# A decoder step on one core: the MLP by Strassen's seven products, the embedding ahead of it, the gate by halves

## The chip, the cores and the metric

One core of a Trainium2 chip. The metric is device time in microseconds (us) from the start to the end of one execution. The engines are named as in the profile: PE (matrix products), DVE and POOL (element by element), ACT (functions, and copies), SP (issues the transfers).

## What is computed

One decoder layer for 1024 prompt tokens and 32 sample tokens, all fp32, width 1024. Attention over a window, a recurrent branch and their mix come first and are not touched. The part that changes:

```python
x = x + mix
hmid = relu(rmsnorm(x, norm2_g) @ w_up)         # 1024 -> 4096
x = x + (hmid * hmid) @ w_down                  # 4096 -> 1024
gate = sigmoid(rmsnorm(x, ple_norm_g) @ w_ple_gate)
x = x + gate * (p @ w_ple)                      # p: 256 wide
```

## The kernel before

Everything is kept feature-major: a matrix of 1024 features by T = 1056 tokens is KT = 8 tiles of 128 features, `X[j]` being the residual. An fp32 product is made of two parts of each operand, high and low: `product` (L234) issues three matmuls for each tile k of the inner dimension, high weights by high tokens (L239), high by low (L240), low by high (L241). `piece` and `linear` (L243, L252) run one group of weights (128 output features) over three chunks of 352 tokens. `weights` hands out a group: it splits the next one (ACT casts the high part, L141, DVE subtracts for the low part, L142), and SP loads the one after that.

Side work is spread by the class `Flow`: `flow.later(n, f)` and `flow.run(generator, n)` put work off by n chunks, and `flow.step()` after each chunk emits what has come due. What is emitted stands in its engine's queue in that order, and each engine works its queue in order.

- **w_out and second norm.** `put_x1` (L1008) adds each chunk to `X`; `with_gain` (L983) squares it and sums the squares on POOL, and splits x times gain into `x1a` and `x1b` (ACT, then DVE). The division by the norm is put off: the MLP works on x times gain, the sums (`mean_square`, L997) come due two chunks into the MLP, and POOL multiplies `X` by them in the first quarter (L1039).
- **MLP.** Four quarters f, each of 8 groups up and 8 groups down, 24 matmuls of 352 columns for a chunk. `put_up` (L1029): ACT relu, POOL square, ACT square to the high part, DVE low part (L1035). `put_down` (L1048): DVE adds the product to `X` (L1050); in the last quarter it multiplies by the norm and calls `with_gain` again, with `x2a` and `x2b`.
- **Gate.** For each row j: 72 matmuls of `w_ple_gate` (`put_gate`, L1118), then 18 of the embedding `w_ple` (`put_y`, L1123), and `write_out` (L1100) turns `X[j]` on PE (L1107), copies it on ACT and sends it. It is put off by one chunk (`flow.run(write_out(...), 1)`, L1155), and a chunk of row j + 1 is emitted ahead of it.

PSUM has two pools of four banks, `pm` for the main products and `po` for the rest.

Of the kernel before, what the change touches and what calls it, by code (L numbers as in the profile page):

```python
# [13 lines left out]
F32 = mybir.dt.float32  # L14
# [12 lines left out]
CH = [(c * CW, CW) for c in range(3)]  # L27
H, G, HD, WIN = 8, 2, 64, 128
# [5 lines left out]
UL = 384                  # width of a row of the biases by distance, u = 255 - distance  # L34
# [26 lines left out]
class Flow:  # L61
    """Work beside the main products, emitted a number of chunks of theirs later."""
# [8 lines left out]
    def run(self, steps, chunks=0):  # L71
        """steps: a generator that yields how many chunks to wait."""
# [17 lines left out]
def trunk(ctx: ExitStack, tc: tile.TileContext, I, O):  # L90
# [25 lines left out]
    def chunk_tmp(tag):  # L116
        return late.tile([P, CW], F32, tag=tag, name=tag, bufs=2)
# [74 lines left out]
    def use_w_ple(j):  # L192
# [5 lines left out]
        def split(raw):  # L198
            w = big.tile([P, 4, P], F32R, tag=("e7", "e0")[j % 2], name="wple")
# [24 lines left out]
    for f in range(FF // D):  # L224
        for i in range(KT):
            use_w(I["w_up"][0], (8 * f + i) * P)
        for j in range(KT):
            use_w(I["w_down"][0], j * P, r0=f * D)
# [28 lines left out]
    def rsqrt(r, ms, u):  # L257
        """r = -2 / sqrt(ms): a first value by logarithm and exponential, then one Newton step."""
# [9 lines left out]
    # -------------------------------------------------------------- constants  # L268
# [7 lines left out]
    # ------------------------------------------------- x, normalised, turned  # L276
# [84 lines left out]
    # --------------------------------------------------------------- k, v, q  # L361
# [61 lines left out]
    def window_out(last, new, which):  # L423
        """The new keys or values, feature-major, to the windows."""
# [32 lines left out]
    # ------------------------------------------------- biases by distance  # L457
# [21 lines left out]
    def biases():  # L479
        # [query, key] views of the biases: distance query + 128 - key  # L480
# [5 lines left out]
        # the samples' rows are (sequence, token, head of the group)  # L486
# [17 lines left out]
    # ------------------------------------------------------ start, keys, values  # L504
# [77 lines left out]
    # A group's values: high parts in the columns of its own partitions, low parts in the others.  # L582
# [22 lines left out]
    # ---------------------------------------------- attention of the prompt  # L605
    def attend():
# [40 lines left out]
        def values(g, b, parts):  # L647
            """High and low values' sums stand on the two halves of the partitions."""
# [36 lines left out]
    # ---------------------------------------------- attention of the samples  # L685
# [76 lines left out]
    # ------------------------------------------- state and decay rates  # L762
    # softplus(-lambda) = 2 atanh(s / (2 - s)) + max(-lambda, 0), s = sigmoid(-|lambda|)
# [73 lines left out]
        # The r and i gates: the input's high part stands on a block's half of the partitions, its low  # L837
        # part on the other half, so a product over all of them takes both.
# [353 lines left out]
```

## Time and profile before

| what | us |
|---|---|
| median of 3 runs (1695.31 to 1698.9) | 1698.87 |
| the profiled execution, its span | 1695.9 |
| PE busy, of the span | 1644.0 (97%) |
| DVE busy | 715.0 (42%) |
| ACT busy | 654.1 (39%) |
| POOL busy | 421.4 (25%) |
| MLP, first matmul of up to last of down | 824 to 1562 |
| gate and embedding, to the end | 1563 to 1696 |

The span is what the profiler saw between the first and the last instruction; the median of the runs is 3.0 us above it. A row of the trace gives start, length, engine, line, operation, output<-inputs and shape; in brackets stands how long the engine had been idle before it, and what released it. The length of a single matmul is its way through the array; successive starts give the time that each costs.

### The profile page before, as it was taken

The page shows a single profiled execution, that of the slowest core. Times are in us where ns is not written, and L with a number is a line of the kernel's source. Part 1 is how long each engine was busy: PE and PEld are TensorE (multiplying, and loading weights), DVE is VectorE, ACT ScalarE, POOL GpSimd, SP SyncE. Part 2 cuts the span into 40 slices and gives each one's busy share as a digit, 9 for nine tenths or more (in the row PEclk, how much of TensorE's full clock was granted, in tenths as well). Part 3 has the DMA queues.
Part 4 walks back from the last instruction along what each step waited for, and adds up shares of the span by engine and source line. Part 5 has one row for each costly group of instructions (what it writes and reads, how often), then busy time and mean ns, then how long its engine had stood idle before and what let it go on. Part 6 is the DMA issues. An engine that isn't in the chain of part 4 may idle for free.

```text
span 1695.9 us, 24877 instructions
## 1 busy us (share of the span) xinstructions
PE 1644.0 (97%) x10283; PEld 1625.5 (96%) x10283; DVE 715.0 (42%) x1155; ACT 654.1 (39%) x1177; POOL 421.4 (25%) x435
## 2 busy tenths in 40 slices
PE   6889999989899999999999999999999999999998
PEld 5889999889899999999999999999999999999998
DVE  5697665574641153333344224222222222355533
ACT  5555656888892223332232013310231013222322
POOL 4462216344530002234453002200120002144000
PEclk9999999999999999999999999999999999999999
DMA  5422112111111123322211111111111111111222
GB/s 169 63 91 67 61 58 79 29 41 44 43 52 50 29 74 103 101 76 80 60 41 48 50 51 38 50 50 40 49 50 45 43 50 41 48 50 54 64 76 61
DMA packets 174570, 100.48 MB, mean 59 GB/s; under 512 B 17396, under 2 KB 171140, under 8 KB 174440
## 3 DMA queue, kind: packets, MB, share of 16 engines
q1 hardware_dynamic: 174456, 98.88, 20.3%
q8 instruction: 81, 1.33, 0.3%
q14 instruction: 33, 0.27, 0.1%
HBM read 88.32 MB, written 11.55 MB: 59 GB/s over the span
## 4 chain that ended last, share of the span: by engine, by line
PE 90%; DVE 5%; DMA 2%; ACT 2%; issue 1%; SPq 0%; ACTq 0%; DVEq 0%
PE m L239 28%; PE m L241 28%; PE m L240 28%; DMA rev<-by_dist 2%; PE m L654 1%; PE o L642 1%; DVE qh L452 1%; DVE xhl L844 1%; DVE hn L265 0%; PE o L239 0%; PE o L240 0%; PE o L241 0%; PE o L619 0%; PE o L620 0%; PE o L1107 0%
## 5 line engine op out<-in xcount | busy, mean ns | idle before, releaser
L239 PE MATMUL m<-xa,wh 128*128 128x352 f32 x912 | 298.8, 328 | 0.0
L240 PE MATMUL m<-xb,wh 128*128 128x352 f32 x912 | 295.9, 324 | 1.1 <-DVE xb L333 1.0
L241 PE MATMUL m<-xa,wl 128*128 128x352 f32 x912 | 295.8, 324 | 0.0
L241 PE MATMUL m<-uh,wl 128*128 128x352 f32 x768 | 248.2, 323 | 0.0
L239 PE MATMUL m<-x1a,wh 128*128 128x352 f32 x768 | 247.9, 323 | 0.0
L239 PE MATMUL m<-uh,wh 128*128 128x352 f32 x768 | 247.7, 323 | 0.0
L240 PE MATMUL m<-ul,wh 128*128 128x352 f32 x768 | 247.6, 322 | 0.0
L240 PE MATMUL m<-x1b,wh 128*128 128x352 f32 x768 | 246.3, 321 | 0.0
L241 PE MATMUL m<-x1a,wl 128*128 128x352 f32 x768 | 246.3, 321 | 0.0
L141 ACT CAST wh<-wraw 128x1024 fp32r<-128x1024 f32 (+1 forms) x126 | 128.2, 1018 | 278.4 <-PE m L240 278.0
L142 DVE TENSOR_TENSOR wl<-wraw,wh 128x1024 fp32r<-128x1024 f32 (+1 forms) x133 | 161.5, 1215 | 145.0 <-ACT wh L141 124.9
L1033 POOL TENSOR_TENSOR rl<-rl 128x352 f32<-128x352 f32 x96 | 81.6, 850 | 544.2 <-ACT rl L1032 544.2
L1035 DVE TENSOR_TENSOR ul<-rl,uh 128x352 fp32r<-128x352 f32 x96 | 68.4, 713 | 256.7 <-POOL rl L1033 256.7
L240 PEld LDWEIGHTS m<-xb,wh 128*128 128x128 f32 x912 | 174.2, 191 | 2.3 <-DVE xb L333 2.0
L239 PEld LDWEIGHTS m<-xa,wh 128*128 128x128 f32 x912 | 174.0, 191 | 0.6 <-ACT xa L332 0.2
L241 PEld LDWEIGHTS m<-xa,wl 128*128 128x128 f32 x912 | 173.6, 190 | 0.0
L240 PEld LDWEIGHTS m<-ul,wh 128*128 128x128 f32 x768 | 144.9, 189 | 0.0
L240 PEld LDWEIGHTS m<-x1b,wh 128*128 128x128 f32 x768 | 144.4, 188 | 0.1
L241 PEld LDWEIGHTS m<-uh,wl 128*128 128x128 f32 x768 | 144.4, 188 | 0.0
L239 PEld LDWEIGHTS m<-x1a,wh 128*128 128x128 f32 x768 | 144.1, 188 | 0.1
L239 PEld LDWEIGHTS m<-uh,wh 128*128 128x128 f32 x768 | 144.2, 188 | 0.0
L241 PEld LDWEIGHTS m<-x1a,wl 128*128 128x128 f32 x768 | 144.0, 188 | 0.0
(310 smaller groups left out, 2809.1 us busy)
## 6 DMA issues: line engine op xcount, KB each, us to landing
wraw<-in_w_in SPq DMA_DIRECT2D x34, 512.0 KB
wraw<-in_w_up SPq DMA_DIRECT2D x32, 512.0 KB
wraw<-in_w_down SPq DMA_DIRECT2D x32, 512.0 KB
s_dram<-sgr SPq DMA_DIRECT2D x8, 528.0 KB
sin<-s_dram SPq DMA_DIRECT2D x8, 528.0 KB
wraw<-in_w_o_rnn SPq DMA_DIRECT2D x8, 512.0 KB
wraw<-in_w_out SPq DMA_DIRECT2D x8, 512.0 KB
xi<-in_x_prompt SPq DMA_DIRECT2D x8, 512.0 KB
```

Source lines behind the costliest of these rows:

```text
L141: high(hi[:, :nk, :], raw[:, :nk, :])
L142: low.tensor_tensor(lo[:, :nk, :], raw[:, :nk, :], f32(hi[:, :nk, :]), op=ALU.subtract)
L239: PE.matmul(ps, wh, xh, start=k == 0, stop=False)
L240: PE.matmul(ps, wh, xl, start=False, stop=False)
L241: PE.matmul(ps, wl, xh, start=False, stop=k == nk - 1)
L452: low.tensor_tensor(both[other], qn[o], f32(both[o]), op=ALU.subtract)
L642: PE.transpose(ps[:, j * WIN:(j + 1) * WIN], S[:, j, kb * WIN:(kb + 1) * WIN], ident)
L654: PE.matmul(ps, vs[g][:, kt, :], part[:, kb, :], start=kb == 0 and part is parts[0], stop=kt == b and part is parts[1])
L844: low.tensor_tensor(xhl[b][other], xc[o], f32(xhl[b][o]), op=ALU.subtract)
L1033: POOL.tensor_tensor(st[:, 1, :n], st[:, 0, :n], st[:, 0, :n], op=ALU.mult)
L1035: DVE.tensor_tensor(ul[i][:, o], st[:, 1, :n], f32(hi), op=ALU.subtract)
```

## The change

- **The normalisation is carried out.** After w_out, `second_norm` makes the sums, the reciprocal root and, for each half of the tokens (528), eight products `xn[j]` = X times gain times norm on DVE (L1086). `with_gain` of the second norm, POOL's product with `X` and the reciprocals are gone.
- **The embedding's product stands ahead of the MLP**: 8 rows by 2 halves by 12 matmuls of 264 columns; ACT copies the results out of PSUM, and they go to DRAM (`e_dram`) until the gate loads them again. `second_norm` is emitted from the fourth chunk of it on.
- **MLP by Strassen.** Eight phases (up and down by f). A phase is the product of a 1024 by 1024 block of weights A with a 1024 by 1056 block of tokens B, each in four quarters, as seven products (`PRODUCTS`) where `product` made eight. A step is one of the seven products and one row tile p of 512: 24 matmuls of 264 columns. 8 phases by 28 steps by 24 are 5376 matmuls of 264, where 4608 of 352 were.
- **Sums and splits for it.** Sums of weight quarters, `w_sums`, 16 in a phase, 512 wide, on POOL in the first and all down phases, on DVE in the other up phases; sums of token quarters, `b_sums`, 16 on DVE in the first and all down phases; splits of weights (28 in a phase: ACT L1151, DVE L1155) and of tokens (28 in the first and the down phases: ACT L1182, DVE L1183). The split tokens of the first phase are written to DRAM (`xc_dram`), and the other up phases load them from there into the ring. `evacuate` (L1227) adds a product to one or two of the four result quarters, on DVE: 40 additions of 528 columns in a down phase; in an up phase 28, and ACT copies besides.
- **Gate.** Halves of the tokens outside, rows j inside; 48 matmuls of 264 for each of 16 steps. The gate weights are all split at the end of the MLP (L1278, L1279, eight groups of 1024 columns). `gate_out` (L1369) works on 528 columns.

```diff
+    flow.run(second_norm(), 4)
+    for j in range(KT):
+        w = weights()
+        for h in range(2):
...
+                product(ps, lambda k: (w[0][:, k, :], w[1][:, k, :]), lambda k: (pa[0][:, k, o], pa[1][:, k, o]), 2)
+                ACT.copy(e[:, c * CQ:(c + 1) * CQ], ps)
+                flow.step()
+            SP.dma_start(e_dram[j, :, HALF[h]], e)
...
+    PRODUCTS = [("A12", "B21"), ("A11", "B11"), ("S2", "T2"), ("S3", "T3"), ("A22", "T4"), ("S1", "T1"), ("S4", "B22")]
...
+        eng = POOL if phases[ph][0] == "down" or ph == 0 else DVE
...
+        for to, op in ([(q11, ALU.add)], [(q11, ALU.add), (q22, ALU.add)], [(q22, ALU.add)],
+                       [(q22, ALU.add), (q12, ALU.subtract)], [(q21, ALU.add)],
+                       [(q22, ALU.add), (q21, ALU.subtract)], [(q12, ALU.add)])[q]:
+            put(to, to, op)
...
+    for s in range(STEPS):
...
+        prepare(s)
...
+        for c in range(2):
+            ps = a[:, c, :CQ]
+            for k in range(4):
+                r = unit(s // 4, k)[:, :, c * CQ:(c + 1) * CQ]
+                PE.matmul(ps, w[:, k, :], r[:, 0, :], start=k == 0, stop=False)
+                PE.matmul(ps, w[:, k, :], r[:, 1, :], start=False, stop=False)
+                PE.matmul(ps, w[:, 4 + k, :], r[:, 0, :], start=False, stop=k == 3)
+        while pending:
+            evacuate(*pending.popleft())
+        pending.append((s, a[:, :, :CQ]))
+        prepare_b(s)
...
+    split_gate(1)
+    for j in range(2, KT):
+        load_gate(j)
+        split_gate(j)
...
+    for th_ in range(2):
+        for j in range(KT):
...
+            for c in range(2):
...
+                if j == 0 and c == 0:
+                    third_norm(th_)
...
+            if not last:
+                gate_out(j, th_, gt, e, a, [0, 1])
+            parts = [(0, 1, 2, 3)] if th_ == 0 else [(6, 7), (8,)] if last else [(4, 5, 6, 7), (8,)]
+            flow.run(write_out(j, parts), 0 if last else 1)
             flow.step()
-            if c < 2 or j == KT - 2:
-                divide()
...
-        for a in held:
-            put_gate(*a)
-        if not last:
-            embedded(put_y)
-            flow.run(write_out(j, [(0, 1, 2, 3), (4, 5, 6, 7), (8,)]), 1)
```

How it moves the instructions on DVE around the second norm: before, from the last chunk of w_out into the MLP (`L1035` is put_up's low part, `L142` a split of weights).

```order
L1010 TENSOR_TENSOR X<-X,m 128x352
L995 SCALAR_TENSOR_TENSOR x1b<-X,vec,x1a 128x352
L142 TENSOR_TENSOR wl<-wraw,wh 128x1024
L1035 TENSOR_TENSOR ul<-rl,uh_7732 128x352 x2
L1002 TENSOR_SCALAR ssq<-o 128x352 x3
L1035 TENSOR_TENSOR ul<-rl,uh_7732 128x352
L142 TENSOR_TENSOR wl<-wraw,wh 128x1024
```

Now (`L212` splits one row's embedding weights, `L268` to `L270` are the Newton step of the root, `L1155` the first split of the MLP's weights, `L1183` of its tokens):

```order
L1066 TENSOR_SCALAR g2h<-vec 128x8
L212 TENSOR_TENSOR wple<-wraw,wple 128x256
L1074 TENSOR_SCALAR ssq<-o 128x352 x3
L268 TENSOR_TENSOR u<-rms,ssq 128x528
L269 TENSOR_TENSOR u<-u,rms 128x528
L270 SCALAR_TENSOR_TENSOR rms<-u,rms 128x528
L1086 SCALAR_TENSOR_TENSOR xn<-X,g2h,rms 128x528 x8
L212 TENSOR_TENSOR wple<-wraw,wple 128x256
L268 TENSOR_TENSOR u<-rms,ssq 128x528
L269 TENSOR_TENSOR u<-u,rms 128x528
L270 SCALAR_TENSOR_TENSOR rms<-u,rms 128x528
L1086 SCALAR_TENSOR_TENSOR xn<-X,g2h,rms 128x528 x8
L212 TENSOR_TENSOR wple<-wraw,wple 128x256 x5
L1155 TENSOR_TENSOR wu<-wblock,wu 128x512
```

The splits of the embedding's rows 2 and 3 now stand behind the eight products of the first and of the second half.

On PE in the gate, before: the last six of a chunk of row 1 (`m_13883`), the four transposes of row 0 (`X_6690`), and the next chunk of row 1.

```order
L239 MATMUL m_13883<-x2a_12881,wh_13804 128x352
L240 MATMUL m_13883<-x2b_12882,wh_13804 128x352
L241 MATMUL m_13883<-x2a_12881,wl_13805 128x352
L1107 MATMUL o_13911<-ident_81,X_6690 128x128 x4
L239 MATMUL m_13923<-x2a_12881,wh_13804 128x352
```

Now (`acc_15684` is row 0's gate, `acc_15766` row 1's):

```order
L1390 MATMUL acc_15684<-x2h_15535,gw_15637 128x264
L1391 MATMUL acc_15684<-x2l_15534,gw_15637 128x264
L1392 MATMUL acc_15684<-x2h_15535,gw_15637 128x264
L1360 MATMUL acc_15756<-ident_87,X_6690 128x128 x4
L1390 MATMUL acc_15766<-x2h_15078,gw_15648 128x264
```

The transposes of row 0 stood behind a chunk of row 1, and now stand directly behind row 0's own last matmul, ahead of all of row 1.

On DVE from the last steps of the MLP to the gate, before:

```order
L1050 TENSOR_TENSOR X<-X,m 128x352
L1052 TENSOR_TENSOR X<-X,ssq 128x352
L995 SCALAR_TENSOR_TENSOR x2b<-X,vec,x2a 128x352
L1002 TENSOR_SCALAR ssq_12880<-o 128x352 x3
L264 TENSOR_TENSOR t<-ssq,ssq_12880 128x352
```

Now (`L1227` adds a product, `L1216` is the low part of the gate's tokens, `L1279` that of a gate weight, `L1348` the third norm's sums, `L1371` the first of `gate_out`):

```order
L1227 TENSOR_TENSOR X<-X,acc 128x528
L1255 TENSOR_TENSOR X<-X 128x528
L1279 TENSOR_TENSOR gw<-graw,gw 128x1024
L1216 SCALAR_TENSOR_TENSOR x2l<-X,vec,x2h 128x528
L1227 TENSOR_TENSOR X<-X,acc 128x528
L1255 TENSOR_TENSOR X<-X 128x528
L1279 TENSOR_TENSOR gw<-graw,gw 128x1024 x7
L1348 TENSOR_SCALAR ssq<-acc 128x528
L268 TENSOR_TENSOR t<-rms_15714,ssq 128x528
L269 TENSOR_TENSOR t<-t,rms_15714 128x528
L270 SCALAR_TENSOR_TENSOR rms_15714<-t,rms_15714 128x528
L1371 TENSOR_TENSOR gt<-acc,rms_15714 128x528
```

The low parts of all eight gate weights now stand between the last product of the MLP and the third norm, which `gate_out` of row 0 needs.

## Rows read from the trace of the kernel before

**Rows 1.** The page: the span, and busy time of each engine.

```profile
span 1695.9 us, 24877 instructions
PE 1644.0 (97%) x10283; PEld 1625.5 (96%) x10283; DVE 715.0 (42%) x1155; ACT 654.1 (39%) x1177; POOL 421.4 (25%) x435
```

**Rows 2.** Windows: length, busy PE, PEld, DVE, ACT, POOL (instructions), PE clock, DMA share, GB/s.

```profile
824.00:1562.00 738.00, 738.00 (x4609) 737.36 (x4608) 231.44 (x309) 169.53 (x280) 142.22 (x149) 1.00 0.16 46
```

**Rows 3.** Timeline of PE, matmuls of 256 columns in attention.

```profile
231.60 0.28 PE L619 MATMUL o<-kh,qh 128*128 128x256 f32 x1
...
232.19 0.28 PE L620 MATMUL o<-kl,qh 128*128 128x256 f32 x1
```

**Rows 4.** Groups by line and shape, DVE: busy, mean ns, idle before.

```profile
L142 DVE TENSOR_TENSOR wl<-wraw,wh 128x1024 fp32r<-128x1024 f32 x125 | 156.0, 1248 | 124.4 <-ACT wh L141 104.3 <-POOL wh L141 17.7
L1050 DVE TENSOR_TENSOR X<-X,m 128x352 f32<-128x352 f32 x96 | 49.9, 520 | 219.8 <-PE m L241 219.8
L995 DVE SCALAR_TENSOR_TENSOR x2b<-X,vec,x2a 128x352 fp32r<-128x352 f32 x24 | 14.1, 587 | 15.8 <-ACT x2a L994 15.8
L1126 DVE TENSOR_TENSOR X<-X,gt 128x352 f32<-128x352 f32 x23 | 12.1, 525 | 0.8
L916 DVE TENSOR_TENSOR rb__5576<-gl,ra 128x1056 fp32r<-128x1056 f32 x8 | 10.0, 1251 | 0.0
L142 DVE TENSOR_TENSOR wl<-wraw,wh 128x512 fp32r<-128x512 f32 x8 | 5.5, 686 | 20.5 <-ACT wh L141 20.5
```

**Rows 5.** Groups by line and shape, ACT.

```profile
L1121 ACT ACTIVATE gt<-gt 128x352 f32<-128x352 f32 x23 | 11.3, 498 | 79.3 <-DVE gt L1120 79.2
L915 ACT CAST ra<-gl 128x1056 fp32r<-128x1056 f32 x8 | 8.6, 1074 | 0.0
L1121 ACT ACT_TABLE_LOAD x1 | 1.3, 1283 | 0.0
```

**Rows 6.** Groups by line and shape, POOL.

```profile
L967 POOL TENSOR_TENSOR sin<-sin,A 128x352 f32<-128x352 f32 x24 | 22.6, 940 | 70.4 <-DVE sin L966 70.4
L1039 POOL TENSOR_TENSOR X<-X,ssq 128x1056 f32<-128x1056 f32 x8 | 19.7, 2463 | 0.0
```

**Rows 7.** Timeline of POOL and DVE in the first quarter of the MLP.

```profile
838.92 2.46 POOL L1039 TENSOR_TENSOR X<-X,ssq 128x1056 f32<-128x1056 f32 x1
838.99 2.77 DVE L1035 TENSOR_TENSOR ul<-rl,uh 128x352 fp32r<-128x352 f32 x1 [3.77 <-POOL rl L1033]
...
843.56 0.53 DVE L1035 TENSOR_TENSOR ul<-rl,uh 128x352 fp32r<-128x352 f32 x1 [0.67 <-POOL rl L1033]
```

**Rows 8.** Timeline of one chunk's chain in the gate.

```profile
1684.93 0.32 PE L241 MATMUL m<-x2a,wl 128*128 128x352 f32 x1
...
1685.29 0.53 DVE L1120 TENSOR_TENSOR gt<-m,ssq 128x352 f32<-128x352 f32 x1 [2.09 <-PE m L241]
...
1686.94 0.53 DVE L1126 TENSOR_TENSOR X<-X,gt 128x352 f32<-128x352 f32 x1
```

**Rows 9.** Groups by line and shape, PE: the transposes on the way out.

```profile
L1107 PE MATMUL o<-ident,X 128*128 128x128 f32 x64 | 9.8, 273 | 1.3 <-DVE X L1126 1.0 <-ACT yo L1108 0.3
```

**Rows 10.** Timeline of PE after a gap at the start.

```profile
26.40 1.94 PE L331 MATMUL o<-ident,cx 128*128 128x128 f32 x8 [3.14 <-DVE cx L319]
...
30.78 0.49 PE L239 MATMUL m<-xa,wh 128*128 128x352 f32 x1
31.07 0.49 PE L240 MATMUL m<-xb,wh 128*128 128x352 f32 x1
```

**Rows 11.** Windows, columns as in rows 2: in that gap, behind it, and a shorter gap.

```profile
25.00:26.00 1.00, 0.00 (x0) 0.00 (x0) 0.84 (x3) 0.00 (x0) 0.29 (x2) 0.67 0.00 0
28.00:32.00 4.00, 4.00 (x16) 4.00 (x15) 3.69 (x4) 3.67 (x8) 2.52 (x3) 0.50 0.58 131
101.00:102.00 1.00, 0.12 (x1) 0.00 (x0) 1.00 (x2) 0.00 (x0) 1.00 (x1) 1.00 0.00 0
```

**Rows 12.** Windows: one with much transfer.

```profile
643.00:644.00 1.00, 1.00 (x8) 1.00 (x7) 0.01 (x1) 0.00 (x0) 0.91 (x1) 1.00 1.09 427
```

More of the change, by code (lines that the diff above doesn't have):

```diff
@@ L223, in trunk @@
             use_w(I[w][0], j * P)
[L224 to L228, printed above, removed]
     for j in range(KT):
-        gate, ple = lambda j=j: use_w(I["w_ple_gate"][0], j * P), lambda j=j: use_w_ple(j)
-        for use in (gate, ple) if j < KT - 1 else (ple, gate):
-            use()
+        use_w_ple(j)
     def product(ps, wk, xk, nk):
@@ new lines, in trunk, with put_x1 @@
+    ones = late.tile([P, P], F32, name="ones")
+    POOL.memset(ones, 1.0)
+    ssq = late.tile([P, T], F32, name="ssq")
+    pa = [left.tile([P, 2, T], F32R, tag=f"ring{i}", name=f"p{i}") for i in range(2)]
+    pb = [left.tile([P, 2, T], F32, tag=f"ring{i}", name=f"p{i}") for i in range(2, 4)]
+    for j in range(KT):
+        if j < KT - 1:
+            flow.run(residual(j + 1))
+        def put_x1(c, t0, n, ps):
+            o = slice(t0, t0 + n)
+            x = X[j][:, o]
+            DVE.tensor_tensor(x, x, ps, op=ALU.add)
+            if j == 0:
+                POOL.tensor_tensor(ssq[:, o], x, x, op=ALU.mult)
+            else:
+                sq = chunk_tmp("t")
+                POOL.tensor_tensor(sq[:, :n], x, x, op=ALU.mult)
+                POOL.tensor_tensor(ssq[:, o], ssq[:, o], sq[:, :n], op=ALU.add)
+        if j == 2:
+            flow.run(embedding(*pa, *pb), 1)
+        linear(lambda k: (mh[k // 4][:, k % 4, :], ml[k]), KT, put_x1)
@@ new lines, in trunk, with mean_square @@
+    for name in ("A12", "A11", "A21", "A22"):
+        load_block(0, name)
+    xn = [None] * KT
+    g2h = late.tile([P, KT], F32, name="g2h")
+    DVE.tensor_scalar(g2h, col("g2", 0, KT), -0.5, None, op0=ALU.mult)
+    HALF = [slice(0, TH), slice(TH, T)]
+    def mean_square(ssq, parts):
+        for o in parts:
+            b = bank()[:, :o.stop - o.start]
+            PE.matmul(b, ones, ssq[:, o], start=True, stop=True)
+            DVE.tensor_scalar(ssq[:, o], b, 1.0 / D, EPS, op0=ALU.mult, op1=ALU.add)
@@ new lines, in b_split, with x2_high @@
+    def b_split(g, k):
+        ph, q = of_product(g)
+        kind, f = phases[ph]
+        r = unit(g, k)
+        if kind == "up" and ph:
+            SP.dma_start(f32(r), xc_dram[4 * q + k])
+            return
+        src = b_view(ph, k, *B_HOME[PRODUCTS[q][1]])
+        ACT.copy(r[:, 0, :], src)
+        DVE.tensor_tensor(r[:, 1, :], src, f32(r[:, 0, :]), op=ALU.subtract)
+        if ph == 0:
+            SP.dma_start(xc_dram[4 * q + k], f32(r))
+    ssq2 = ssq
+    x2h = {}
+    def x2_high(j, th_):
+        if (j, th_) not in x2h:
+            m, p = j // 4, j % 4
+            row, half = {(0, 0): (p, 1), (1, 0): (p + 4, 0), (1, 1): (p, 0), (0, 1): (p + 4, 1)}[m, th_]
+            x2h[j, th_] = left.tile([P, TH], F32R, tag=f"h{row}{half}", name="x2h")
+        return x2h[j, th_]
@@ new lines, in split_gate, with prepare @@
+    def split_gate(j):
+        if j < 4:
+            i = place[NPH - 1, ("A21", "A22", "A11", "A12")[j]]
+            w = right.tile([P, 2, KT, P], F32R, tag=f"w{i}", name="gw")
+        else:
+            w = left.tile([P, 2, KT, P], F32R, tag=f"ring{j - 4}", name="gw")
+        gw.append(w)
+        ACT.copy(w[:, 0], raw_gate[j])
+        DVE.tensor_tensor(w[:, 1], raw_gate[j], f32(w[:, 0]), op=ALU.subtract)
+    def prepare(s):
+        if 0 <= s + 6 < STEPS:
+            w_sums(s + 6)
+        if 0 <= s + 5 < STEPS:
+            w_high(s + 5)
+        if 0 <= s + 4 < STEPS:
+            w_low(s + 4)
@@ new lines, in trunk, with third_norm @@
+    while pending:
+        evacuate(*pending.popleft())
+    split_gate(1)
+    for j in range(2, KT):
+        load_gate(j)
+        split_gate(j)
+    rms = {}
+    yp, ys = O["y_prompt"][0], O["y_sample"].rearrange("b t d -> (b t) d")
+    def third_norm(th_):
+        o = HALF[th_]
+        a = acc.tile([P, 2, 512], F32, tag="acc", name="acc")
+        for c in range(2):
+            oc = slice(o.start + c * CQ, o.start + (c + 1) * CQ)
+            PE.matmul(a[:, c, :CQ], ones, ssq2[:, oc], start=True, stop=True)
+        DVE.tensor_scalar(ssq2[:, o].rearrange("p (c n) -> p c n", c=2), a[:, :, :CQ], 1.0 / D, EPS, op0=ALU.mult, op1=ALU.add)
+        ACT.preload_act_table_set("natural_log_exp_and_others")
+        rms[th_] = wpool.tile([P, TH], F32, tag="wraw", name="rms3")
+        rsqrt(rms[th_], ssq2[:, o], chunk_tmp("t"))
@@ new lines, in gate_out @@
+    def gate_out(j, th_, gt, e, a, cs):
+        o = slice(HALF[th_].start + cs[0] * CQ, HALF[th_].start + (cs[-1] + 1) * CQ)
+        og = slice(cs[0] * CQ, (cs[-1] + 1) * CQ)
+        n = len(cs)
+        v = lambda t: t.rearrange("p (c n) -> p c n", c=n)
+        DVE.tensor_tensor(v(gt[:, og]), a[:, cs[0]:cs[-1] + 1, :CQ], v(rms[th_][:, og]), op=ALU.mult)
+        ACT.activation(gt[:, og], gt[:, og], AF.Sigmoid, scale=-0.5)
+        DVE.tensor_tensor(gt[:, og], gt[:, og], e[:, og], op=ALU.mult)
+        DVE.tensor_tensor(X[j][:, o], X[j][:, o], gt[:, og], op=ALU.add)
```

347 lines of the change are left out of this document (224 added, 123 removed).

## The prediction

> **What bounds the kernel now.** I read the page first: PE is busy for 97% of the span, DVE for 42% [rows 1]. Then the MLP by itself, as a window: 738.00 us with PE busy for all of it at full clock, DVE for 231 us and DMA engines for 0.16 of their time [rows 2]. So the product's columns are the time there, 738.00 / 4609 = 0.160 us for 352 columns, and fewer columns are worth their full time as long as the other engines keep up. That condition is the question of this case, since Strassen's sums and the splits go to DVE and POOL. Then the timelines of the gate's chain and of the clock, where the change puts PE behind a chain.
>
> **Durations.** Matmuls of 264 columns are not in the trace. 256 columns cost (232.19 - 231.60) / 5 = 0.118 us [rows 3] and 352 cost 0.160; between them 264 come to 0.1215. On DVE, 352 and 1056 columns take 0.525 and 1.251 us [rows 4], so 528 take 0.706; from PSUM by the same slope from 0.520, 0.70; with a scalar and a tensor, from 0.587, 0.77. ACT takes 0.498 and 1.074 [rows 5], so 0.64. POOL takes 0.940 and 2.463 [rows 6], so 1.29 for 512. All sums are made against the span of the profiled execution, 1695.9; the median of the runs is 3.0 above it.
>
> **A. The MLP's products: -84.2.** 5376 x 0.1215 = 653.2 for 737.4. The bounds are the cost by columns alone (0.160 x 264 / 352 = 0.120, -92) and no saving at all for the shorter form (0.160, +123). I take the interpolation, as 256 columns is the nearest row. The Trainium skill, in "TensorE: Matmul & The Clock Gate", section "Back-to-back issue gap", gives some 81 ns for 128 columns and 131 ns for 512 in a stream of weight loads and matmuls; a straight line between them, my estimate, would be 99 ns for 264 and 110 for 352, and by it the MLP would become 23 us longer instead of shorter. The trace does not agree (0.118 and 0.160 at 256 and 352 columns), and the measurement decides.
>
> **B. Gate and embedding products: +1.4.** 960 x 0.1215 for 720 x 0.160.
>
> **C. The embedding ahead of the MLP: +28.** Its 192 matmuls are 23.3 us, 2.92 for a row. The second norm used to be hidden: its sums came due in the MLP, and nothing waited. Now it stands on DVE between the splits of the embedding's rows 1 and 2. For a half: three sums (1.55), a table load and two functions on ACT (1.28 + 1.28), the Newton step (2.2), eight products (6.1), the split (0.42), together 12.9; they begin about 3 us into the embedding, so row 2 starts at 16.1, where PE could at 6.9. The second half puts 8.7 more ahead of row 3, which starts at 25; then five rows of 2.92. The embedding ends at 39.6 instead of 23.3: +16.3. I add 4 for POOL's sums meeting DVE's products (below), 2.6 for one fall of the clock (G), and 5.2 for the change to the first Strassen product, whose token ring lies where the embedding's operands were, so its first splits wait for the last embedding matmul (two splits on ACT and DVE, 0.64 and 0.71 each, then the weights'). Bounds: 0, if the waits all overlap, and 32.
>
> **D. DVE in the phases that it must feed: +14.** In a down phase DVE has 28 splits of weights (0.686), 28 of tokens (0.706), 16 sums (0.706) and 40 additions (0.70): 78.4 us beside 28 x 2.916 = 81.6 of PE. It fits by 4% if nothing delays DVE. But POOL's 16 sums (20.6 us) lie beside it. The trace shows what that does: while POOL ran its product of 2.46, DVE's subtraction with two operands in SBUF took 2.77, against 0.53 a little later when POOL was idle [rows 7]. Additions out of PSUM are not held in this way, as far as the rows go. Some 8 of the 16 sums come due at the end of the up phase, where DVE has room. If all 20.6 us held DVE, a phase would be 99 us and lose 17.4. I take 3 us in each down phase and 2 in the first up phase, since the ring is one product deep and takes up part of it. Bounds 0 and 40. The Trainium skill, in "SBUF — State Buffer", section "SBUF: two separate sides", has a lock between POOL and a two-input DVE instruction, held for the whole instruction. The trace agrees (2.77 beside 2.46 us), and by that rule at its worst four down phases would lose 70 us instead of 12.
>
> Transfers are no term: an up phase loads 28 x 540 KB and 4.2 MB in 82 us, some 235 GB/s, and the trace has a window with 427 [rows 12].
>
> **E. From the MLP to the gate: +30.** In the last down phase each of four steps also has two preparations of the gate's tokens: two additions (1.40), a sum (0.71), then ACT and DVE by turns (four times 0.64, 0.77 behind), 5.6, with the weights' split 6.3 on DVE's queue for 2.92 on PE. That leaves DVE some 14 us behind, and the last four steps of 3.5 add to it, so the split of the first gate weights (1.25 [rows 4]) is done about 20 us after PE has finished. Then DVE has seven more splits of 1.25 ahead of the third norm, and `gate_out` of row 0 waits for it: about 10 more. Before, the same place held a chain too, but with embedding and gate products beside it. Bounds 12 and 35.
>
> **F. The gate: +48.4.** The four transposes of row j stand on PE directly behind row j's own matmuls, so PE must wait until X is ready. The chain is in the trace for 352 columns: matmul ends at 1685.25, X at 1687.47, 2.22 us [rows 8]. Before, a chunk of another row lay in between, and 64 transposes cost only 1.3 us of waiting [rows 9]. For 528 columns the four operations grow from 2.08 to 2.76 and the wait to 2.9 to 3.05. 15 stalls x 3.05 = 45.8, and 2.6 for the third norm of the second half. There is no cover: what stands behind the transposes in PE's queue is all of row j + 1. Bounds 43 and 50.
>
> **G. The clock: +36.** At the start PE had nothing to do for 3.14 us [rows 10]. Within the gap the mean granted clock of one microsecond was 0.67, and four microseconds of dense matmuls behind it ran at 0.50 [rows 11], the lower of the two levels (1.2 and 2.4 GHz), at 0.29 us for 352 columns instead of 0.160 [rows 10]. PE had gone on at 26.40 [rows 10], so it ran some 5 us at half, and a gap costs some 2.6 us besides itself. In a shorter gap, of which a window shows 0.12 busy, the clock stayed at 1.00 [rows 11]. The gate's gaps of 3.05 are like the first. 14 of 16 at 2.6 are 36; bounds 0 and 47.
>
> **The sum.** -84.2 + 1.4 + 28 + 14 + 30 + 48.4 + 36 = +73.6, a span of 1769.5, with 3.0 above it **1772 us**, slower by 4.3%.
>
> **Rivals.**
>
> R1, **the clock holds in the gate**: a gap of 3.05 between 5.8 us of matmuls need not act like one with none before it. For it: the gap without a fall [rows 11]. Against: 3.14 us did it. G vanishes: 1736, and 1708 with C at nothing.
>
> R2, **DVE bounds the down phases**: POOL's sums hold all of DVE's two-input work. For it: 2.77 against 0.53 [rows 7], and only 3 us of slack in a phase. Against: half of the sums fall elsewhere, and additions from PSUM pass. D becomes 40 to 70: 1798 to 1828.
>
> R3, **the preparation runs ahead of PE, and the change gains**. The place is the queue of splits on ACT and DVE. If it stays a product ahead as the weights do now (PE 738.00 of 738.00 busy [rows 2]), C, D and E vanish: -72, which gives 1700; and with no fall of the clock in the gate 1664. It decides when C, D, E and G together stay under 34 us, as A and B give 82.8 and F takes 48.4 of them. Against it: the order on DVE itself, where splits stand behind the norm and behind the last evictions. Middle 1682.
>
> R4, **matmuls of 264 cost as much as those of 352**: +207 for the MLP and 37 for the rest, about 2016. Against it: 256 at 0.118 [rows 3].
>
> **How the numbers follow.** Forecast 0.60, R1 0.15, R2 0.11, R3 0.11, R4 0.03. The forecast by itself spans 1740 to 1800. The range of 8 in 10 leaves out R3, R4 and the far part of R2: 1708 to 1815. About 0.2% is what a measurement of this kernel can tell from no change. Faster by more than that: R3 nearly whole and the edge of R1, 0.12; within it 0.03; slower 0.85.
>
> **What would show it.** A: starts of matmuls in the new MLP 0.12 apart wherever PE does not wait. C: PE idle some 9 us before the embedding's third row, and again before the fourth. D: DVE over 90% busy in down phases, two-input work there longer than 0.71 while POOL runs, PE waiting for DVE at L1155 or L1183. E: a gap of some 20 us of PE ahead of the first gate matmul. F: fifteen waits of about 3 us of PE for DVE's last addition to X. G: the granted clock at 0.5 behind them. It is wrong if the gate's PE runs through (F), if the clock there is 1.00 (G, R1), or if down phases last over 95 us (R2).

## The result, and the profile after

The changed kernel takes 1773.78 us (median of 4 runs, 1759.56 to 1775.05) where the kernel before took 1697.09 beside it: ratio 1.044, 95% interval 1.040 to 1.048. The forecast was 1772, slower. Three of the four runs lie between 1772.91 and 1775.05 and one at 1759.56, so a distance of 2 us from the forecast is less than two runs of this kernel differ by. One of late_out's ten runs below took 4599 us; it counts in the median, not in the ratio, and without it the median is 1691.66. The profiled execution has a span of 1773.2, 77.3 above that of before.

The page of the kernel after: span, busy time, and PE's busy tenths and granted clock in 40 slices.

```profile
span 1773.2 us, 28069 instructions
PE 1622.4 (91%) x11293; PEld 1598.5 (90%) x11293; DVE 1037.5 (59%) x1607; ACT 817.5 (46%) x1457; POOL 425.1 (24%) x388
...
PE   6889999899999999999699999999999999847776
...
PEclk9999999999999999999799999999999999968877
```

PE is no longer busy throughout [rows 1]: 91% for 97%, with DVE at 59%. It has a dip in the middle (slice 20, the embedding) and a low stretch at the end (the gate), and the clock is low just there.

Windows of the kernel after, columns as in rows 2: first up phase, a middle up and a middle down phase, the last down phase, half of the gate.

```profile
879.00:963.00 84.00, 80.60 (x613) 79.35 (x614) 74.91 (x100) 51.52 (x90) 31.46 (x20) 0.94 0.61 231
1046.00:1130.00 84.00, 84.00 (x691) 84.00 (x690) 49.52 (x74) 38.59 (x64) 11.77 (x8) 1.00 0.58 210
1130.00:1214.00 84.00, 84.00 (x691) 84.00 (x691) 74.27 (x115) 35.53 (x63) 10.34 (x8) 1.00 0.23 77
1465.00:1557.00 92.00, 83.33 (x650) 82.57 (x649) 84.06 (x114) 40.51 (x69) 27.22 (x18) 0.95 0.04 12
1592.00:1680.00 88.00, 66.59 (x410) 65.21 (x411) 16.15 (x23) 11.10 (x17) 0.00 (x0) 0.79 0.17 49
```

The middle phases run like the MLP before [rows 2]: PE busy for all of 84 us, 691 matmuls in them, 0.122 us for each, with DVE at 59% (up) and 88% (down). The saving of the seven products is there. It is given back in the first and the last phase, ahead of them, and above all in the gate, where PE is busy for 76% of the time at a granted clock of 0.79.

Timeline of PE after, its waits: the embedding and the start of the MLP, the last phase, the gate.

```profile
850.19 0.59 PE L245 MATMUL m<-p,wple 128*128 128x264 f32 x1 [10.37 <-DVE wple L212]
860.24 0.59 PE L245 MATMUL m<-p,wple 128*128 128x264 f32 x1 [4.88 <-DVE wple L212]
878.91 0.39 PE L1318 MATMUL acc<-ring,wu 128*128 128x264 f32 x1 [2.04 <-ACT ring L1182]
...
1522.15 0.56 PE L1318 MATMUL acc<-ring,wu 128*128 128x264 f32 x1 [4.03 <-DVE X L1227]
...
1553.13 0.36 PE L1318 MATMUL acc<-ring,wu 128*128 128x264 f32 x1 [3.25 <-DVE X L1227]
...
1566.24 0.59 PE L1390 MATMUL acc<-x2h,gw 128*128 128x264 f32 x1 [8.51 <-ACT gw L1278]
1569.19 0.59 PE L1392 MATMUL acc<-x2h,gw 128*128 128x264 f32 x1 [2.14 <-DVE gw L1279]
1592.05 1.08 PE L1360 MATMUL acc<-ident,X 128*128 128x128 f32 x4 [13.56 <-DVE X L1374]
1603.06 1.09 PE L1360 MATMUL acc<-ident,X 128*128 128x128 f32 x4 [3.05 <-DVE X L1374]
1615.25 0.63 PE L1360 MATMUL acc<-ident,X 128*128 128x128 f32 x4 [3.05 <-DVE X L1374]
```

Each wait names what it was for: the embedding's low parts, an eviction, the gate's weights, and then, row after row, `X` from `gate_out`: seven waits of 3.05, one of 4.59 with the third norm, six of 2.94, and two of 2.01 for the last row. The group says it in one row, 61.2 us with row 0's 13.56, where the same transposes had waited 1.3 [rows 9].

Groups of the kernel after, PE.

```profile
L1360 PE MATMUL acc<-ident,X 128*128 128x128 f32 (+1 forms) x72 | 17.5, 376 | 61.2 <-DVE X L1374 61.2
```

Timeline of DVE and POOL after, in the embedding and in the last phase.

```profile
840.25 9.55 DVE L1086 SCALAR_TENSOR_TENSOR xn<-X,g2h,rms 128x528 f32<-128x528 f32 x8
...
842.80 6.44 POOL L1140 TENSOR_TENSOR wblock<-wblock 128x512 f32<-128x512 f32 x4 [8.18 <-DMA wblock<-in_w_up]
...
849.73 0.41 DVE L212 TENSOR_TENSOR wple<-wraw,wple 128x256 fp32r<-128x256 f32 x1
...
1513.86 3.53 DVE L1172 TENSOR_TENSOR hid<-hid 128x528 f32<-128x528 f32 x2
1515.07 6.84 POOL L1146 TENSOR_TENSOR s<-wblock,s 128x512 f32<-128x512 f32 x4
...
1541.12 3.07 POOL L1208 TENSOR_TENSOR ssq<-ssq,t 128x528 f32<-128x528 f32 x2 [4.65 <-ACT t L1207]
...
1541.64 3.12 DVE L1216 SCALAR_TENSOR_TENSOR x2l<-X,vec,x2h 128x528 fp32r<-128x528 f32 x2 [0.72 <-ACT x2h L1215]
```

The split L212, 0.41 us long, stands behind eight products and starts at 849.73; PE goes on at 850.19. Where POOL works, DVE's instructions with two operands in SBUF take 1.2 to 1.8 us instead of about 0.7.

Groups of DVE after: the token splits of a middle down phase (1134.57 to 1216.52), and the gate's low parts in the last one (1462.36 to 1557.70).

```profile
L1183 DVE TENSOR_TENSOR ring<-hid,ring 128x528 fp32r<-128x528 f32 x24 | 18.1, 773 | 2.0 <-ACT ring L1182 1.9
...
L1216 DVE SCALAR_TENSOR_TENSOR x2l<-X,vec,x2h 128x528 fp32r<-128x528 f32 x12 | 16.3, 1381 | 4.5 <-ACT x2h L1215 4.5
```

So POOL hardly holds DVE in the middle phase (0.77 us for about 0.71), and holds it in the last (1.38 for about 0.77).

The clock falls outside the gate's rows too. Timeline of PE in row 2 of the gate, at half clock, and the window of row 0's 48 matmuls:

```profile
1604.39 0.42 PE L1392 MATMUL acc<-x2h,gw 128*128 128x264 f32 x1
1604.61 0.42 PE L1390 MATMUL acc<-x2h,gw 128*128 128x264 f32 x1
```

```profile
1566.24:1578.49 12.25, 10.11 (x52) 9.39 (x52) 10.21 (x11) 6.12 (x7) 1.44 (x1) 0.65 0.43 128
```

At half clock a matmul of 264 columns costs 0.220 us, at full clock 0.122, so 1 us of busy PE at half clock is 0.445 us lost. Summed over the stretches where the granted clock is 0.50, PE is busy for 9.1 us in the embedding, 9.7 in the first phase, 14.8 from the last phase's first matmul to row 0's transposes, and 68.1 from there to the end: 4.1, 4.3, 6.6 and 30.3 us lost.

One stretch that the change hardly touches also differs: all ahead of the MLP and the embedding ended at 824.2 before and at 831.8 after. Some 2 us are the transposes of the embedding's input, which now lie there. The rest comes and goes between executions of one and the same code: among the profiled runs below, the first embedding matmul starts between 823.2 and 832.0, and the granted clock at the start and in the recurrent stage tells the late ones from the early.

Windows of the start and of the recurrent stage, after (late) and with the edit gate_split (early; its edit is far behind these places).

```profile
25.00:32.00 7.00, 5.90 (x23) 5.93 (x24) 5.97 (x7) 4.21 (x8) 2.89 (x4) 0.52 0.33 75
300.00:500.00 200.00, 183.47 (x1103) 180.57 (x1102) 114.99 (x121) 170.35 (x240) 88.67 (x74) 0.97 0.15 42
```

```profile
25.00:32.00 7.00, 5.92 (x37) 5.09 (x38) 6.06 (x7) 4.12 (x8) 3.71 (x4) 1.00 0.33 75
300.00:500.00 200.00, 183.43 (x1132) 180.53 (x1131) 115.05 (x120) 174.82 (x245) 91.19 (x75) 0.99 0.16 44
```

So I compare profiles by the **main stretch**, from the first embedding matmul (before: from the first MLP matmul) to the end: 871.7 us before, 941.4 after. It is one execution of each, and even there stretches that no edit touches differ: from row 0's transposes to the end 181.2 us in the change and 178.2 with pool_split. A difference of 3 us in the main stretch says little by itself; where one matters below, I give the stretch in which it arises.

### The profile page after: what moved, and what is told of

The parts are those of the page before. It is cut to its first block, busy times and chain, and to the rows that moved or that the text cites. A ratio compares the mean times of both kernels' runs of the same rounds, so it can differ in the third digit from the quotient of the medians.

```text
span 1773.2 us, 28069 instructions
## 1 busy us (share of the span) xinstructions
PE 1622.4 (91%) x11293; PEld 1598.5 (90%) x11293; DVE 1037.5 (59%) x1607; ACT 817.5 (46%) x1457; POOL 425.1 (24%) x388
## 4 chain that ended last, share of the span: by engine, by line
PE 79%; DVE 13%; ACT 3%; DMA 3%; issue 2%; SPq 0%; DVEq 0%; ACTq 0%
PE m L243 11%; PE m L245 11%; PE acc L1319 11%; PE m L244 11%; PE acc L1320 11%; PE acc L1318 11%; PE acc L1390 2%; PE acc L1391 2%; PE acc L1392 2%; DMA rev<-by_dist 2%; DVE x2l L1216 1%; DVE xn L1086 1%; PE acc L1360 1%; DVE X L1227 1%; DVE ring L1183 1%
## 5 line engine op out<-in xcount | busy, mean ns | idle before, releaser
L1318 PE MATMUL acc<-ring,wu 128*128 128x264 f32 x1792 | 512.9, 286 | 10.5 <-DVE X L1227 8.1
L1319 PE MATMUL acc<-ring,wu 128*128 128x264 f32 x1792 | 515.6, 288 | 3.6 <-DVE ring L1183 3.6
L1320 PE MATMUL acc<-ring,wu 128*128 128x264 f32 x1792 | 511.6, 285 | 0.0
L1318 PEld LDWEIGHTS acc<-ring,wu 128*128 128x128 f32 x1792 | 340.1, 190 | 11.5 <-issue 7.6
L1319 PEld LDWEIGHTS acc<-ring,wu 128*128 128x128 f32 x1792 | 340.3, 190 | 5.1 <-DVE ring L1183 5.1
L1320 PEld LDWEIGHTS acc<-ring,wu 128*128 128x128 f32 x1792 | 341.4, 190 | 0.0
L1151 ACT CAST wu<-wblock 128x512 fp32r<-128x512 f32 x160 | 98.8, 618 | 197.3 <-PE acc L1320 179.1
L153 DVE TENSOR_TENSOR wl<-wraw,wh 128x1024 fp32r<-128x1024 f32 (+1 forms) x61 | 71.4, 1171 | 120.8 <-ACT wh L152 102.8
L1155 DVE TENSOR_TENSOR wu<-wblock,wu 128x512 fp32r<-128x512 f32 x160 | 117.3, 734 | 15.7 <-ACT wu L1151 15.7
L1227 DVE TENSOR_TENSOR hid<-hid,acc 128x528 f32<-128x528 f32 x112 | 77.1, 700 | 77.4 <-PE acc L1320 51.8
L1227 DVE TENSOR_TENSOR X<-X,acc 128x528 f32<-128x528 f32 x160 | 107.5, 696 | 24.0 <-PE acc L1320 23.6
L1390 PE MATMUL acc<-x2h,gw 128*128 128x264 f32 x256 | 89.3, 349 | 8.5 <-ACT gw L1278 8.5
L1183 DVE TENSOR_TENSOR ring<-hid,ring 128x528 fp32r<-128x528 f32 x112 | 87.6, 802 | 9.7 <-ACT ring L1182 9.6
L1392 PE MATMUL acc<-x2h,gw 128*128 128x264 f32 x256 | 85.2, 333 | 2.1 <-DVE gw L1279 2.1
L1391 PE MATMUL acc<-x2l,gw 128*128 128x264 f32 x256 | 85.9, 335 | 0.0
```

The source lines that it names most:

```text
L1155: DVE.tensor_tensor(units[u][:, 4:, :], w_view(ph, PRODUCTS[q][0], p), f32(units[u][:, :4, :]), op=ALU.subtract)
L1183: DVE.tensor_tensor(r[:, 1, :], src, f32(r[:, 0, :]), op=ALU.subtract)
L1227: put = lambda to, of, op: DVE.tensor_tensor(to, of, ps, op=op)
L1318: PE.matmul(ps, w[:, k, :], r[:, 0, :], start=k == 0, stop=False)
L1319: PE.matmul(ps, w[:, k, :], r[:, 1, :], start=False, stop=False)
L1320: PE.matmul(ps, w[:, 4 + k, :], r[:, 0, :], start=False, stop=k == 3)
```

## The experiments

Each is the changed kernel with one edit, except where several are named.

**late_out**: the transposes one step later.

```diff
-            flow.run(write_out(j, parts), 0 if last else 1)
+            flow.run(write_out(j, parts), 0 if last else 2)
```

> The change with one edit: the transposes of row j are emitted one step later, behind the matmuls of row j+1. Theory (F and G: PE waits for gate_out because the transposes stand directly behind the row's own matmuls, and the waits lower the clock): the waits of 3 us at L1360 vanish but for the first and the last, the granted clock in the gate is 1.00 from the second row on, and the time falls by 46 (waits) + 35 (clock) = 81 us against the change, to about 1693 (1685 to 1703). Rival (the chain on DVE and ACT or the reload of the embedding takes over as the bound of a row): a row stays at 9 us or more and the time falls by less than 40.

Measured: 1692.58 us, ratio to before 0.9978 (0.9964 to 0.9993); 81.2 below the change. Main stretch 862.8, 78.6 less. Group and window of late_out:

```profile
L1360 PE MATMUL acc<-ident,X 128*128 128x128 f32 (+1 forms) x72 | 11.5, 289 | 13.0 <-DVE X L1374 13.0
```

```profile
1600.00:1680.00 80.00, 80.00 (x661) 79.81 (x660) 30.46 (x43) 19.13 (x35) 0.00 (x0) 1.00 0.28 83
```

The waits shrink from 61.2 to 13.0 (7.8 of it at row 0), and in this window PE is busy throughout at full clock. One number in the code is worth 4.6% of the run, and without the stalls the change is no loss any more.

**fill_gap**: matmuls in the waits, so that only PE's idleness goes.

```diff
-            ps = acc.tile([P, 2, 512], F32, tag="acc", name="acc")[:, 0, :]
+            pt = acc.tile([P, 2, 512], F32, tag="acc", name="acc")
+            ps = pt[:, 0, :]
...
+            if len(tt) == 4:
+                for i in range(24):
+                    PE.matmul(pt[:, 1, :CQ], gw[0][:, 0, i % 8, :], x2_high(i % 8, 0)[:, :CQ], start=True, stop=True)
```

> The change with PE kept busy in the gate's waits: ahead of the four transposes of a row stand 24 matmuls of 264 columns into an unused bank (2.9 us), whose results nobody reads. The waits' time stays, only the idleness goes. Theory (G is caused by PE's gaps, and is a cost beside them): the granted clock in the gate goes to 1.00, a row takes 5.85 + 2.95 + 0.5 = 9.3 us instead of 11.5, and the time falls by 30 to 35 us, to about 1741. Rival (the clock is low there for another reason than the gaps): clock stays near 0.78, the fill costs its time at half clock too, and the time is the same or higher.

Measured: 1741.52, 32.3 less than the change (main stretch 27.1 less). Window of the gate's first half with it:

```profile
1585.00:1680.00 95.00, 93.30 (x739) 91.28 (x740) 22.48 (x32) 15.67 (x24) 0.00 (x0) 0.98 0.19 57
```

The clock goes from 0.79 to 0.98. More work on PE made the kernel faster: the low clock is a cost of the gaps beside their length. From row 0's transposes to the end 27.7 us are gained, and 7.0 us of busy PE at half clock are left (3.1 us lost); together this is the 30.3 that the half clock cost there in the change, to within 0.5. This parts F from G, and late_out's gain is both.

**pool_split**: the embedding's low parts on POOL.

```diff
-            DVE.tensor_tensor(w[:, 2:4, :], raw, f32(w[:, 0:2, :]), op=ALU.subtract)
+            POOL.tensor_tensor(w[:, 2:4, :], raw, f32(w[:, 0:2, :]), op=ALU.subtract)
```

> The change with the low parts of the embedding's weights made on POOL instead of DVE, so that they no longer stand behind the second norm's products on DVE. Theory (C: two waits of PE, 10.4 and 4.9 us, are for these splits): both waits shrink below 3 us, the first Strassen matmul comes 12 to 20 us earlier behind the first matmul of the embedding (47.1 us in the change), the time falls by as much, to about 1757. Rival (the second norm bounds the start of the MLP itself, whose first splits stand behind its second half on DVE): the waits move to the first Strassen product, and the time falls by less than 6.

Measured: 1755.8; main stretch 929.2, 12.2 less, the low edge of what was expected; the first Strassen matmul comes 34.6 us behind the first of the embedding, for 47.1. PE's waits there, then ACT ahead of the wait of 4.08, then POOL and DVE at the start of the MLP:

```profile
845.10 0.59 PE L243 MATMUL m<-p,wple 128*128 128x264 f32 x1 [4.08 <-ACT e L1099]
864.87 0.59 PE L1318 MATMUL acc<-ring,wu 128*128 128x264 f32 x1 [2.04 <-ACT ring L1182]
867.06 0.59 PE L1319 MATMUL acc<-ring,wu 128*128 128x264 f32 x1 [1.61 <-DVE ring L1183]
...
844.37 0.41 ACT L211 CAST wple<-wraw 128x256 fp32r<-128x256 f32 x1 [5.29 <-DMA wraw<-in_w_ple]
844.68 1.21 ACT L1099 COPY e<-m 128x264 f32<-128x264 f32 x4
...
863.50 6.36 POOL L1142 TENSOR_TENSOR s<-wblock 128x512 f32<-128x512 f32 x4
863.80 1.52 DVE L1155 TENSOR_TENSOR wu<-wblock,wu 128x512 fp32r<-128x512 f32 x1 [10.24 <-ACT wu L1151]
865.24 3.47 DVE L1183 TENSOR_TENSOR ring<-xn,ring 128x528 fp32r<-128x528 f32 x2
```

The waits for L212 are gone, so they were DVE's order. What is left is new. PE waits 4.1 us for ACT's copies out of PSUM, and these stand on ACT behind the cast of a row's weights, which waits 5.29 us for their load. And in the first product there are 3.6 us of waits for DVE (1.61, 0.68 and 1.28), where the change had 1.5: POOL's sums of weights come later now, behind the low parts, and DVE's first splits take 1.5 to 1.8 us beside them. The second norm, which was the rival, is not what is left: DVE had been idle for 10.24 us before its first split.

**gate_split**: the third norm ahead of six of the splits.

```diff
     split_gate(1)
-    for j in range(2, KT):
-        load_gate(j)
-        split_gate(j)
+    load_gate(2)
+    load_gate(3)
...
                 gate_out(j, th_, gt, e, a, [0, 1])
+            if th_ == 0 and j + 2 < KT:
+                split_gate(j + 2)
+                if j + 4 < KT:
+                    load_gate(j + 4)
```

> The change with the gate weights 2 to 7 split row by row inside the first half of the gate instead of all ahead of it, so that the third norm stands behind two splits instead of eight. Theory (E: gate_out of row 0 waits for the third norm, and that for the splits): the wait of 13.6 us ahead of the first transposes shrinks by 6 x 1.25 = 7.5 us, to about 6, and the time falls by 7 to 10, to about 1765. Rival (the third norm waits for the sums of squares on POOL, or for ACT's backlog): the wait stays above 11 us and the time the same.

Measured: 1757.69; main stretch 931.1, 10.3 less. The wait at row 0:

```profile
1576.85 1.09 PE L1359 MATMUL acc<-ident,X 128*128 128x128 f32 x4 [5.07 <-DVE X L1373]
```

It is 5.07 for 13.56, 8.5 less: the eight splits did stand in the way. From the first gate matmul to row 0's transposes it is 16.8 us for 25.8, 9.0 less.

**sums_dve_last** and **sums_dve_all**: sums of weights off POOL, in the last and in all down phases.

```diff
-        eng = POOL if phases[ph][0] == "down" or ph == 0 else DVE
+        eng = POOL if phases[ph][0] == "down" and ph < NPH - 1 or ph == 0 else DVE
...
+        eng = POOL if ph == 0 else DVE
```

> The change with the last down phase's 16 sums of weights on DVE instead of POOL. DVE gets 16 x 0.71 = 11.3 us of work more and loses what POOL's sums cost it. Theory (POOL's sums hold DVE's two-input work: 1.8 instead of 0.7 us beside them): the wait of 4.0 us for DVE's addition to X in the last phase shrinks below 1, DVE's other instructions return to 0.7, and the time falls by 2 to 5 us. Rival (that wait is DVE's load alone): the wait grows, and the time rises by 3 to 8 us.

> The change with the sums of weights of all down phases on DVE. Theory (D: the middle down phases have 4% to spare, and half of the sums fall into the up phase ahead): DVE is busy for about 80 of 82 us in a middle down phase, PE still does not wait there, and the time differs from sums_dve_last by less than 3 us. Rival (the down phases are at DVE's limit): waits of 2 us and more in each down phase, and 6 to 20 us more.

Measured: 1765.49 and 1766.4; main stretch 938.5 and 937.8, 2.9 and 3.6 less. From the last phase's first matmul to the gate's first it is 102.0 in both for 103.9, so 1.9 us are due to the edit (the traces that leave this place alone have 103.6 to 104.0); most of the rest lies in the first phase, which takes 89.8 to 92.0 us without any edit there. This is just under the 2 to 5 that I had expected. In the last phase the wait of 4.03 is gone, and two of 1.39 and 1.20 for token splits came: 11.3 us more work on DVE gained 1.9. With all of them on DVE, a middle down phase:

```profile
1130.00:1214.00 84.00, 84.00 (x691) 84.00 (x691) 77.97 (x126) 30.55 (x52) 0.00 (x0) 1.00 0.29 99
```

DVE is busy for 78.0 of 84, POOL for none, and PE still does not wait. The middle phases are not bound by DVE, with POOL's sums or without them.

**three_edits**: late_out, pool_split and gate_split together.

> The edits of late_out, pool_split and gate_split together. They act at three places one behind another, so theory: the gains add up but for a part of gate_split's, since late_out has already given the wait at row 0 some cover: 1692.6 - 18 - 6 = 1668 (1660 to 1676), 1.6% below the kernel before. Rival (the places hide one another, the same DVE backlog being paid at the next of them): above 1685.

Measured: 1677.91, ratio to before 0.9892 (0.9871 to 0.9913); just above the range that was expected. Main stretch 848.6, 92.8 less than the change, for 101.1 of the three apart. The overlap lies behind the first gate matmul: late_out alone leaves a wait of 7.82 at row 0, so gate_split had less to shorten, and new waits of 0.68 and 1.79 came behind it.

**early_gate**: the three edits, and the gate's first two weights split ahead of the last products.

```diff
-        if s == STEPS - 4:
+        if s == STEPS - 28:
             load_gate(0)
             load_gate(1)
-        elif s == STEPS - 1:
+        elif s == STEPS - 15:
             split_gate(0)
+        elif s == STEPS - 11:
+            split_gate(1)
+        elif s == STEPS - 4:
+            load_gate(2)
+            load_gate(3)
...
-    split_gate(1)
```

> The three edits, and the first two gate weights loaded at the start of the last down phase and split in its fourth and fifth products instead of at its end. Theory (E: the wait of 8.4 us ahead of the first gate matmul is for the split of its weights, which on ACT stands behind the gate's tokens): the waits of 8.4 and 2.1 us vanish and 6 to 10 us are gained on three_edits, to about 1660. Rival (DVE's backlog as such bounds the gate's start, the split is only the last to come): the wait moves to a low part x2l or to the third norm, and less than 3 us are gained.

Measured: 1674.13, ratio 0.9873 (0.9854 to 0.9892). But the main stretch is 848.9 against 848.6, so nothing was gained there; the rest is the stretch ahead. PE's waits:

```profile
1545.08 0.39 PE L1394 MATMUL acc<-x2h,gw 128*128 128x264 f32 x1 [1.04 <-DVE X L1227]
1549.29 1.13 PE L1351 MATMUL acc<-ssq,ones 128*128 128x264 f32 x4 [1.00 <-DVE X L1227]
1565.52 1.09 PE L1364 MATMUL acc<-ident,X 128*128 128x128 f32 x4 [6.07 <-DVE X L1378]
```

The waits of 8.17 and 2.14 in three_edits are gone, but counted from the first embedding matmul the gate starts only 3.3 us earlier (1545.08 - 823.76 against 1553.55 - 828.95), as DVE's two splits now lie in the last phase; and then PE waits 6.07 for `gate_out`, where three_edits has no wait at row 0. My theory fell, the rival held: the weights were only the last to come. DVE's backlog from the last eight steps is what is left: it adds the MLP's last product to `X` at 1556.71, 13 us after PE began the last matmul of it (1543.76), and the third norm comes behind.

**high_first**: early_gate, and on ACT the gate's high part ahead of the square.

```diff
         x, o = X[j][:, HALF[th_]], HALF[th_]
+        g, hi = col("g3", j), x2_high(j, th_)
+        ACT.activation(hi, x, AF.Identity, scale=g)
...
-        g, hi = col("g3", j), x2_high(j, th_)
-        ACT.activation(hi, x, AF.Identity, scale=g)
```

> early_gate with the gate's tokens prepared in another order on ACT: the high part first, then the square for the norm. Theory (what bounds the end of the last phase is DVE and ACT working by turns: DVE stands 1.40 us before each low part, for a square and a high part): DVE's wait before L1216 falls from 1.40 to about 0.75, the evictions of the last eight steps come earlier, and 4 to 6 us are gained from the embedding's start to the end (848.9 us in early_gate). Rival (the bound is what DVE executes, POOL's sums beside it included): DVE's low parts get longer by what the wait gets shorter, and less than 1.5 us are gained.

Measured: 1673.35, ratio 0.9872 (0.9857 to 0.9886), the same as early_gate within the runs' spread; main stretch 845.0, 3.9 less, and 4.2 less from the last phase's first matmul to row 0's transposes (115.7 for 119.9), where the edit acts. One of the low parts in early_gate, and the corresponding one in high_first:

```profile
1547.16 1.37 DVE L1216 SCALAR_TENSOR_TENSOR x2l<-X,vec,x2h 128x528 fp32r<-128x528 f32 x1 [1.40 <-ACT x2h L1215]
```

```profile
1550.48 0.77 DVE L1216 SCALAR_TENSOR_TENSOR x2l<-X,vec,x2h 128x528 fp32r<-128x528 f32 x1 [0.80 <-ACT x2h L1206]
```

The wait is 0.80 for 1.40, as expected, and the instruction itself 0.77 for 1.37, since POOL's sum, which follows the square, no longer falls on it. It falls on the next addition to `X` (L1255) instead, which takes 1.1 us for 0.71. The turns of DVE and ACT were part of E.

**all_five**: high_first and sums_dve_last.

> high_first with the last phase's sums of weights on DVE too (sums_dve_last, which gained 3.0 us from the embedding's start to the end). Theory: these act at the start and the end of the same phase, so they add up: 3 us less than high_first, about 1667, and the wait of 4.9 us for DVE's addition at 1507 us vanishes. Rival (DVE is the bound all through the last phase, so that its added 11.3 us come out later): the same time as high_first or more.

Measured: 1676.95 (1668.68 to 1678.86), ratio 0.9898 (0.9881 to 0.9914); main stretch 843.7, 1.3 less than high_first, for 3 expected. The wait of 4.9 is replaced by waits of 1.15, 0.77 and 2.52 for DVE earlier in the phase. The median is not below high_first's; the runs do not tell the two apart.

The versions with three edits and more beat both kernels, that of before by 1.0% to 1.3%.

## Why the prediction was right, point by point

The direction, the time (1773.78 for 1772) and the places were right; the sum owes part of its closeness to luck. E and the stretch ahead of the embedding came out 12 and 8 us above the forecast, C, D, F and G each 4 to 6 below it, and most of the 8 comes and goes between executions. Measured in the two profiled executions:

| term | forecast | measured | from |
|---|---|---|---|
| A, MLP products | -84.2 | -81.8 | 0.12195 a matmul over 224 in a middle phase, x 5376 |
| B, gate and embedding products | +1.4 | +1.9 | the same, x 960 |
| C, embedding ahead | +28 | +23.7 | 47.1 from 831.8 to 878.9, less 23.4 |
| D, first and middle phases | +14 | +9.8 | all in the first phase |
| E, MLP to gate | +30 | +41.9 | 13.1 in the last phase, 8.8 to the gate, 20.0 at row 0 |
| F, waits in the gate | +48.4 | +43.6 | 14 waits behind row 0 |
| G, clock in the gate | +36 | +30.3 | 68.1 of busy PE at half clock from 1592.05 on, x 0.445 |
| ahead of the embedding | 0 | +7.6 | 831.8 against 824.2 |
| end and transposes | 0 | +0.3 | the rest |

- **A** held, and with it the interpolation from 256 and 352 columns [rows 3]; R4 fell. So did my straight line between the two figures of the Trainium skill, "TensorE: Matmul & The Clock Gate", section "Back-to-back issue gap": 0.122 us was measured at 264 columns, where that estimate gave 0.099.
- **C** held in mechanism (pool_split took both waits away) and was 4 too high: the gaps were 10.4 and 4.9, together 15.3 for the 16.3 that I had, with POOL's contention already in them; the 4 that I added for it were one too many. The change to the first Strassen product cost a wait of 2.04 for my 5.2, and two falls of the clock 4.1 for my 2.6; some 2 us of the 23.7 stay without a name. (The row that I had start at 6.9 without the norm would have started at 5.8, two rows of 2.92; the sum does not use it.)
- **D** was mis-sized. I charged the middle down phases 3 us each; they lost nothing. The step that failed is what POOL's sums do to DVE there. Half of them fall into a down phase, as I had said (10.3 us in the window from 1130 to 1214), but they cost DVE little (0.77 us for a token split), and DVE was busy for 74.3 of 84, 88% where I had expected over 90%. R2 fell with it, sums_dve_all showing the room that was left. In the first phase, the ring was late instead (waits up to 1.5 us for L1183), and the half clock (0.94 on average) cost 4.3 of the 9.8.
- **E** was 12 too low, beyond its bound of 35. Its waits are 32.9 us for 30 forecast (8.7 in the last phase, 10.7 at the gate's first matmuls, 13.6 at row 0), so the step that failed is a term that I had put at nothing: the clock falls in this passage as it does in the gate, and cost 6.6; some 2 us stay without a name. The chain at its base was right (DVE and ACT by turns in the last steps, high_first), but I left POOL's work out of it: it stretched DVE's two-input instructions there to 1.4 to 1.8, and DVE was busy for 84.06 of the window's 92 us; moving the sums of weights off POOL gave 1.9 back. And I named the gate's weights as the wait; early_gate shows that they were only its last link, and the gap of 20 us that I expected ahead of the first gate matmul was 8.5, the other waits coming earlier.
- **F** held: seven waits of 3.05 and six of 2.94, for 3.05, and 4.59 with the third norm, for 5.65. They are 14 where I had counted 15, as the last row's two of 2.01 stand under the end and row 0's in E.
- **G** held for the gate: behind each of the 14 gaps the clock fell, and fill_gap took 27.7 us off there by keeping PE busy. It came out 6 below: the fourteen cost 27.0 us, 1.9 each for my 2.6. R1 fell, but the one row on which I had rested the rule [rows 10] would have spoken for R1 in another execution (last section).
- **R3** fell: C, D, E and G together were 105.7, far above its 34. With the gate's stalls gone and C and E shortened the change does gain: high_first's main stretch is 845.0 against 871.7 before.

## What to carry to other kernels

Saved columns on the bound engine pay only where all others keep up, and a phase-by-phase window tells that quickly: here six of eight phases did, and the loss lay in the passages. Where work is emitted a fixed number of steps later, a change of the step's size or the loop's order can put an engine directly behind its own chain; look at what stands behind the instruction in the queue, and move it one step on. And a gap of PE of some 3 us can cost more than its length, for the clock may fall: in the gate of the change it did behind 14 of 14.

## What was not expected of the hardware

Code that is the same in all of these kernels took up to 9 us longer in some executions than in others, and the granted clock tells where. At the start PE has a gap ahead of the same transposes in all of them. It was 3.12 us in the change, and the clock from 25 to 32 us was 0.52; in gate_split it was 3.13 us, and the clock stayed at 1.00 (the windows in the section on the result). So one gap of about 3 us does not settle whether the clock falls, and G's premise came from an execution in which it did. In the recurrent stage PE's gaps are about 2.2 us long, between the 1.4 us that let the clock be before (101.11 to 102.49) [rows 11] and the 3.1; some of them lower it and some don't (0.97 or 0.99 over 200 us). In pool_split one of the gate's gaps of 3.05 us (to 1603.28) left the clock at 1.00 as well. What decides it stays open.

In the gate of the change, gaps of about 3 us between stretches of PE at work lowered the clock each time. But PE was then busy at half clock for 3.1 to 5.9 us, where it was for 5.6 us or more at the start [rows 10, 11]. So one gap cost 2.6 us beside its length (ahead of row 2, 12.2 us from gap to gap) and the next one 1.5 (ahead of row 3, 11.1 us).
